# Loads and stores of the down weights' sums issued by GpSimd instead of SyncE, in the forgetting-attention loop of a YOCO-style trunk

## The chip, the cores and the metric

The kernel runs on one core of one Trainium2 chip. The metric is the device time of one execution in microseconds (us), the median of three runs. A core has five engines with instruction streams of their own: TensorE (PE in the profile, with its weight loads as PEld), VectorE (DVE), ScalarE (ACT), GpSimd (POOL) and SyncE (SP). In this kernel DMAs are issued by SP and by POOL; each of the two has a queue of its own, and all transfers share the core's 16 DMA engines. An instruction that waits holds up everything behind it on its engine.

## What is computed

Two layers of a decoder trunk over 512 tokens of width 1024: a dilated windowed attention with a gated ConvFFN, then a shared key/value projection, the forgetting attention (FoX) and a second ConvFFN. The change lies in the loop of the forgetting attention. Cut to that:

```python
def fox_mixer(xn, w_q, w_o, k, v, c):
    q = (xn @ w_q).reshape(B, T, B_HEADS, HEAD_DIM)          # 16 heads of 64
    for i in range(T // BLK):                                # 4 blocks of 128 queries
        s = einsum(q[block], k[:prefix]) * scale
        s = s + (c_t[:, :, q0:q1, None] - c_t[:, :, None, :q1])   # forget bias
        s = where(causal, s, NEG)
        p = softmax(s)
        outs.append(einsum(p, v[:prefix]))
    return concat(outs) @ w_o

def conv_ffn(xn, w_up, cw, cb, w_down):
    ...
    return (gelu(gate) * val) @ w_down
```

The kernel's second ConvFFN needs, besides `w_down` itself, differences of blocks of `w_down` (the "down weights' sums"). They depend on nothing but the weights, so they are made ahead, during the attention loop, and kept in a DRAM tile `dT[1]`.

## The kernel before, in words

**The loop.** 16 heads are taken as 8 pairs j = 0..7, and the 4 query blocks as two halves (i0 = 0 and 2), which makes 16 *steps* m = 0..15: step m works on j = m // 2 and i0 = 0 (m even) or 2 (m odd), each step with two sub-steps a = 0, 1 (query block i = i0 + a). Two more rounds (m = 16, 17) drain the pipeline. In one step PE does scores (L1715, `s_ps`), the probability-value products of step m - 2 (L1762, `o_ps`), four parts of the next heads' query projection (`q_part`, through `mm3` L277 to L279, `q_ps`) and the transposes of step m - 1's probabilities (L1747, `pT_ps`). DVE adds the bias and finds the minimum (L1723), ACT does the exponential (L1725), DVE divides (L1735), ACT copies the transposes (L1749).

**The bias.** `f_bias` (L1690 and after) runs on POOL, one step ahead: for each sub-step two TENSOR_SCALARs (L1696) and one AFFINE_SELECT (L1697). The first bias of an even step has 128x384 operands, its second one 128x512; in an odd step they are 128x128 and 128x256. They read `ck`, a broadcast copy of the cumulative gate for pair j, 512 KB, which SP loads at the start of each even step (L1492).

**The weights.** Products are done in three passes with a high and a low part of each weight. Query weights come in pieces of 512 KB: SP loads `wraw` (L49); ACT writes the high part (L57) and the negated high part (L59, `high(minus=True)`, end of an even step); then, in the next odd step, POOL issues a DMA that *adds* `wraw` onto the negated part, which gives the low part (`low_added`, L82). This is called the **accumulate** below. The accumulate issued in odd step m is used by PE in step m + 1, sub-step 1: in `q_part` the first product of the group that needs the low part is L279. So the accumulates of steps 1, 3, 5, 7, 9 are wanted in steps 2, 4, 6, 8, 10; that of step 11 belongs to the output projection and is wanted later.

**The sums.** `sums_between(l, j)` is a generator: it loads 1 MB of `w_down` in three DMAs (L1783 512 KB, L1784 and L1785 256 KB each) into a tile `dsums`, then on DVE makes four subtractions (L1787, L1788; L1790, L1791), then stores 1 MB into `dT` (L1793). Four of them run in the loop, for j = 2..5, started at m = 2, 6, 10, 14:

```python
for j, m in ((2, 2), (3, 6), (4, 10), (5, 14)):
    g = sums_between(1, j)
    for i in ((m, 1), (m + 1, 2), (m + 2, 0), (m + 2, 1)):
        sums[i] = g
```

so the loads stand at (m, sub-step 1), the subtractions at the end of step m + 1 and in step m + 2, sub-step 0, and the store at (m + 2, sub-step 1); all of m, m + 2 are even. In the loop's body `next(sums.get((m, a), idle))` comes right behind `f_bias` and `q_part` of that sub-step.

**What sets the order.** The program is scheduled by hand: each engine's order is the order of the code. Tiles come from pools with a fixed number of buffers (`t4`: 10 of 4 KB a partition, for `wraw`, `ck` and `bias`; `t8`: 16 of 8 KB, for `w`, `dsums` and others), so an instruction that fills a tile also waits for the last readers of what the buffer held. The second bias of an even step gets the buffer of the `wraw` that the preceding accumulate reads, and so waits for that accumulate to land.

Of the kernel before, what the change touches and what calls it, by code (L numbers as in the profile page):

```python
# [101 lines left out]
def trunk_kernel(ctx, tc, x, norm_gains, w_qkv_a, w_o_a, w_q_b, w_o_b, kv_norm, w_kvf, b_f,  # L102
                 w_up, conv_w, conv_b, w_down, rope, out):
    nc = tc.nc
    act, dve, pool, pe, sp = nc.scalar, nc.vector, nc.gpsimd, nc.tensor, nc.sync
# [8 lines left out]
    def t8(shape, dt=F32, name="t8"):  # L114
        return p8.tile(shape, dt, tag="t8", name=name)
# [47 lines left out]
    dT = [tc.dram_tile([ND, 128, 2048], F32, name=f"dT{l}") for l in range(2)]  # L163
# [1472 lines left out]
    for bp in range(2):  # L1636
        for s in range(2):
            t = slice(bp * 128, bp * 128 + 128)
# [139 lines left out]
    def sums_between(l, j):  # L1778

        t = t8([128, 2, 1024], name="dsums")  # L1780
        a, b = t[:, 0], t[:, 1]
        r = w_down[l][j * 256:j * 256 + 256, :].rearrange("(c p) d -> c p d", p=128)
        sp.dma_start(a, r[0])  # L1783
        sp.dma_start(b[:, 0:512], r[1, :, 512:1024])  # L1784
        sp.dma_start(b[:, 512:1024], r[1, :, 0:512])  # L1785
        yield
        dve.tensor_tensor(a[:, 0:512], a[:, 512:1024], a[:, 0:512], ALU.subtract)  # L1787
        dve.tensor_tensor(a[:, 512:1024], b[:, 0:512], a[:, 512:1024], ALU.subtract)  # L1788
        yield
        dve.tensor_tensor(b[:, 0:512], b[:, 0:512], a[:, 0:512], ALU.subtract)  # L1790
        dve.tensor_tensor(b[:, 512:1024], b[:, 512:1024], b[:, 0:512], ALU.subtract)  # L1791
        yield
        sp.dma_start(dT[l][j].rearrange("p (q d) -> p q d", q=2), t)  # L1793
        yield

    pairs = [(j, i) for j in range(8) for i in (0, 2)]
# [13 lines left out]
# [4 lines that stand above are left out]
    for m in range(M + 2):  # L1814
        live = m < M
        if live:
            j, i0 = pairs[m]
# [91 lines left out]
```

## Time and profile before

| | |
|---|---|
| median of 3 runs | 1118.66 us (1118.03 to 1118.78) |
| the profiled execution's own time | 1118.55 us |
| its span (first to last instruction) | 1116.8 us, so 1.75 us lie around it |
| busy: PE, PEld, DVE, ACT, POOL | 1100.9, 949.9, 895.5, 660.8, 212.8 us |
| mean granted TensorE clock | 0.996 |
| the attention loop's steps in the trace | about 619 to 737 us |
| DMA moved | 237.32 MB, mean 213 GB/s |

The page gives shares of the whole span. The change touches some 110 us of it, so the views that matter are those cut to that stretch: the waits of one engine, its instructions in order of time, the chain of work that ended last, and the busy time of each engine and of the DMA engines in windows. In a row of the instruction view stand start, duration, engine, line, operation and tiles, and in square brackets the idle time before it with what ended it. In a row of the windows stand the window, its length, the busy time of PE, PEld, DVE, ACT and POOL (with instruction counts), the granted clock, the DMA engines' mean busy share and GB/s.

### The profile page before, as it was taken

The page shows a single profiled execution, that of the slowest core. Times are in us where ns is not written, and L with a number is a line of the kernel's source. Part 1 is how long each engine was busy: PE and PEld are TensorE (multiplying, and loading weights), DVE is VectorE, ACT ScalarE, POOL GpSimd, SP SyncE. Part 2 cuts the span into 40 slices and gives each one's busy share as a digit, 9 for nine tenths or more (in the row PEclk, how much of TensorE's full clock was granted, in tenths as well). Part 3 has the DMA queues.
Part 4 walks back from the last instruction along what each step waited for, and adds up shares of the span by engine and source line. Part 5 has one row for each costly group of instructions (what it writes and reads, how often), then busy time and mean ns, then how long its engine had stood idle before and what let it go on. Part 6 is the DMA issues. An engine that isn't in the chain of part 4 may idle for free.

```text
span 1116.8 us, 18134 instructions
## 1 busy us (share of the span) xinstructions
PE 1100.9 (99%) x6611; PEld 949.9 (85%) x6611; DVE 895.5 (80%) x1494; ACT 660.8 (59%) x1092; POOL 212.8 (19%) x313
## 2 busy tenths in 40 slices
PE   9999999999999999999999899999999999999997
PEld 6988889899999988887988677788989999988886
DVE  6667778878888799997877577858978877799995
ACT  5444565656556557476555577756565565557473
POOL 1832101111111111000110555500211111111000
PEclk9999999999999999999999899999999999999999
DMA  9469854468788989794882666583457889899862
GB/s 324 151 216 407 334 163 134 112 148 192 187 183 201 297 303 337 264 336 78 206 183 64 207 190 190 169 244 101 119 141 176 197 206 217 234 319 334 314 245 76
DMA packets 185075, 237.32 MB, mean 213 GB/s; under 512 B 11737, under 2 KB 131529, under 8 KB 184474
## 3 DMA queue, kind: packets, MB, share of 16 engines
q1 hardware_dynamic: 169274, 185.00, 51.0%
q0 software_dynamic: 15712, 51.16, 20.9%
q8 instruction: 52, 0.85, 0.3%
q14 instruction: 37, 0.30, 0.1%
HBM read 170.28 MB, written 39.63 MB: 188 GB/s over the span
## 4 chain that ended last, share of the span: by engine, by line
PE 84%; issue 6%; DMA 4%; ACT 3%; DVE 2%; POOL 1%; DVEq 0%; POOLq 0%; ACTq 0%; SPq 0%
PE up L278 13%; PE up L277 13%; PE up L279 13%; PE acc L278 8%; PE acc L277 8%; PE acc L279 8%; DMA w<-wraw 3%; PE qk_ps L278 2%; PE qk_ps L277 2%; PE qk_ps L279 2%; PE first L279 1%; PE first L277 1%; PE first L278 1%; PE v_ps L277 1%; PE v_ps L279 1%
## 5 line engine op out<-in xcount | busy, mean ns | idle before, releaser
L277 PE MATMUL acc<-w 128*128 128x512 f32 (+1 forms) x311 | 120.5, 388 | 0.0
L279 PE MATMUL acc<-w 128*128 128x512 f32 (+1 forms) x311 | 120.4, 387 | 0.0
L57 ACT CAST w<-wraw 128x1024 fp32r<-128x1024 f32 x96 | 99.1, 1048 | 14.1 <-DMA wraw<-in_w_o_b_dram 5.3
L278 PE MATMUL acc<-w 128*128 128x512 f32 (+1 forms) x267 | 103.3, 387 | 0.0
L65 DVE TENSOR_TENSOR w<-wraw,w 128x1024 fp32r<-128x1024 f32 x66 | 88.2, 1351 | 18.4 <-ACT w L57 17.8
L641 ACT ACTIVATE bb<-up,conv 128x512 f32<-128x512 f32 x80 | 60.0, 775 | 67.4 <-DVE up L1022 42.8
L278 PE MATMUL up<-xbl,w 128*128 128x512 f32 (+1 forms) x280 | 96.3, 344 | 0.0
L278 PE MATMUL up<-xcl,w 128*128 128x512 f32 (+1 forms) x280 | 96.3, 344 | 0.0
L277 PE MATMUL up<-xch,w 128*128 128x512 f32 (+1 forms) x280 | 96.3, 344 | 0.0
L277 PE MATMUL up<-xbh,w 128*128 128x512 f32 (+1 forms) x280 | 96.3, 344 | 0.0
L279 PE MATMUL up<-xch,w 128*128 128x512 f32 (+1 forms) x280 | 96.2, 344 | 0.0
L279 PE MATMUL up<-xbh,w 128*128 128x512 f32 (+1 forms) x280 | 96.2, 344 | 0.0
L279 PE MATMUL up<-xsh,w 128*128 128x256 f32 x320 | 90.6, 283 | 0.0
L277 PE MATMUL up<-xsh,w 128*128 128x256 f32 x320 | 90.6, 283 | 0.0
L278 PE MATMUL up<-xsl,w 128*128 128x256 f32 x320 | 90.6, 283 | 0.0
L277 PEld LDWEIGHTS acc<-w 128*128 128x128 f32 x311 | 58.4, 188 | 12.0
L279 PEld LDWEIGHTS acc<-w 128*128 128x128 f32 x311 | 58.4, 188 | 11.8
L644 DVE SCALAR_TENSOR_TENSOR bb<-up,conv,bb 128x510 f32<-128x510 f32 x80 | 59.9, 749 | 2.8
L277 PEld LDWEIGHTS up<-xsh,w 128*128 128x128 f32 x320 | 61.4, 192 | 0.0
L278 PEld LDWEIGHTS up<-xsl,w 128*128 128x128 f32 x320 | 61.4, 192 | 0.0
L279 PEld LDWEIGHTS up<-xsh,w 128*128 128x128 f32 x320 | 61.4, 192 | 0.0
L642 DVE SCALAR_TENSOR_TENSOR bb<-up,conv,bb 128x511 f32<-128x511 f32 x80 | 59.4, 742 | 2.6 <-ACT bb L641 2.6
(333 smaller groups left out, 3154.2 us busy)
## 6 DMA issues: line engine op xcount, KB each, us to landing
wraw<-in_w_up_dram SPq DMA_DIRECT2D x88, 512.0 KB, 5.2
w<-wraw POOLq DMA_DIRECT2D x50, 512.0 KB, 6.0
dT<-dsums SPq DMA_DIRECT2D x24, 512.0 KB, 6.5
dsums<-in_w_down_dram SPq DMA_DIRECT2D x22, 512.0 KB, 5.4
dsums<-in_w_down_dram SPq DMA_DIRECT2D x44, 256.0 KB, 7.2
hD<-hc POOLq DMA_DIRECT2D x44, 256.0 KB, 7.8
dact<-hD SPq DMA_DIRECT2D x44, 256.0 KB, 5.6
wraw<-dT SPq DMA_DIRECT2D x22, 512.0 KB, 6.6
```

Source lines behind the costliest of these rows:

```text
L57: self.nc.scalar.copy(pair[:, 0], raw)
L65: self.nc.vector.tensor_tensor(pair[:, 1], raw, pair[:, 0].bitcast(F32), ALU.subtract)
L277: pe.matmul(o, ah, bh, start=first, stop=False, skip_group_check=shared)
L278: pe.matmul(o, ah, bl, start=False, stop=False, skip_group_check=shared)
L279: pe.matmul(o, al, bh, start=False, stop=last, skip_group_check=shared)
L641: act.activation(bb[:, s, :], ps, AF.Identity, bias=cp[:, 3, ch:ch + 1], scale=cp[:, 2, ch:ch + 1])
L642: dve.scalar_tensor_tensor(bb[:, s, 1:], ps[:, :T - 1], cp[:, 1, ch:ch + 1], bb[:, s, 1:], ALU.mult, ALU.add)
L644: dve.scalar_tensor_tensor(bb[:, s, 2:], ps[:, :T - 2], cp[:, 0, ch:ch + 1], bb[:, s, 2:], ALU.mult, ALU.add)
```

## The change

The four DMA issues of `sums_between` go from `sp` to `pool`; the generator's places in the loop stay. It runs four times, so 12 loads (4 MB) and 4 stores (4 MB) move.

```diff
@@ sums_between
-        sp.dma_start(a, r[0])
-        sp.dma_start(b[:, 0:512], r[1, :, 512:1024])
-        sp.dma_start(b[:, 512:1024], r[1, :, 0:512])
+        pool.dma_start(a, r[0])
+        pool.dma_start(b[:, 0:512], r[1, :, 512:1024])
+        pool.dma_start(b[:, 512:1024], r[1, :, 0:512])
...
-        sp.dma_start(dT[l][j].rearrange("p (q d) -> p q d", q=2), t)
+        pool.dma_start(dT[l][j].rearrange("p (q d) -> p q d", q=2), t)
```

PE, DVE and ACT keep their order to the instruction. On SP, from the query weights' and `ck`'s loads of step 2 on, the rows before are:

```order
L49 DMA wraw<-in_w_q_b_dram 128x8x128
L1492 DMA ck<-cd 128x1024
L1783 DMA dsums<-in_w_down_dram 128x1024
L1784 DMA dsums<-in_w_down_dram 128x512
L1785 DMA dsums<-in_w_down_dram 128x512
L49 DMA wraw<-in_w_q_b_dram 128x8x128
L1492 DMA ck<-cd 128x1024
L1793 DMA dT_76<-dsums 128x2048
L49 DMA wraw<-in_w_q_b_dram 128x8x128
L1492 DMA ck<-cd 128x1024
```

and of the change, from the same row on:

```order
L49 DMA wraw<-in_w_q_b_dram 128x8x128
L1492 DMA ck<-cd 128x1024
L49 DMA wraw<-in_w_q_b_dram 128x8x128
L1492 DMA ck<-cd 128x1024
L49 DMA wraw<-in_w_q_b_dram 128x8x128
L1492 DMA ck<-cd 128x1024
```

The loads and the store are gone from between SP's other loads; a `wraw` load that stood behind a store now stands behind a `ck` load.

On POOL, from the biases of step 2 (rows L1696 and L1697) over the accumulate of step 3 (L82) to that of step 5, the rows before are:

```order
L1696 TENSOR_SCALAR bias<-ck,cq 128x512 x2
L1697 AFFINE_SELECT bias<-bias 128x2x128
L82 DMA w<-wraw 128x1024
L1696 TENSOR_SCALAR bias<-ck,cq 128x128 x2
L1697 AFFINE_SELECT bias<-bias 128x2x128
L1696 TENSOR_SCALAR bias<-ck,cq 128x256 x2
L1697 AFFINE_SELECT bias<-bias 128x2x128
L1696 TENSOR_SCALAR bias<-ck,cq 128x384 x2
L1697 AFFINE_SELECT bias<-bias 128x2x128
L1696 TENSOR_SCALAR bias<-ck,cq 128x512 x2
L1697 AFFINE_SELECT bias<-bias 128x2x128
L82 DMA w<-wraw 128x1024
```

and of the change, at its two ends (first the biases of step 2 and the accumulate of step 3, then the biases of step 4 and the accumulate of step 5):

```order
L1696 TENSOR_SCALAR bias<-ck,cq 128x512 x2
L1697 AFFINE_SELECT bias<-bias 128x2x128
L1783 DMA dsums<-in_w_down_dram 128x1024
L1784 DMA dsums<-in_w_down_dram 128x512
L1785 DMA dsums<-in_w_down_dram 128x512
L82 DMA w<-wraw 128x1024
```

```order
L1696 TENSOR_SCALAR bias<-ck,cq 128x512 x2
L1697 AFFINE_SELECT bias<-bias 128x2x128
L1793 DMA dT_76<-dsums 128x2048
L82 DMA w<-wraw 128x1024
L1696 TENSOR_SCALAR bias<-ck,cq 128x128 x2
L1697 AFFINE_SELECT bias<-bias 128x2x128
```

The loads stand between the second bias of an even step and the next accumulate, and so does the store two steps later. From step 12 on there is no accumulate behind them: the store of step 12 stands ahead of the biases of step 13, and the loads of step 14 and the store of step 16 end POOL's part of the loop.

## The prediction

> **What bounds the kernel now.** The page's first part says that PE is busy 1100.9 of 1116.8 us, so only what stops or slows PE can be won. Next I read who PE waited for in the stretch that the change touches (620 to 700 us), and then those waits in PE's order of time; in the waits' rows stand the total, the count and the longest.
>
> ```profile
> PE 1100.9 (99%) x6611; PEld 949.9 (85%) x6611; DVE 895.5 (80%) x1494; ACT 660.8 (59%) x1092; POOL 212.8 (19%) x313
> ...
> PE q_ps L279 <- DMA w<-wraw: 6.5, 3, 4.9
> ```
>
> ```profile
> 637.83 0.79 PE L279 MATMUL q_ps<-xqh,w 128*128 128x512 f32 x1 [4.91 <-DMA w<-wraw]
> ...
> 653.36 0.40 PE L279 MATMUL q_ps<-xqh,w 128*128 128x512 f32 x1
> ...
> 667.29 0.50 PE L279 MATMUL q_ps<-xqh,w 128*128 128x512 f32 x1 [0.83 <-DMA w<-wraw]
> ...
> 680.33 0.40 PE L279 MATMUL q_ps<-xqh,w 128*128 128x512 f32 x1
> ...
> 694.67 0.50 PE L279 MATMUL q_ps<-xqh,w 128*128 128x512 f32 x1 [0.74 <-DMA w<-wraw]
> ```
>
> These five rows are the first products that need the accumulated low part, in steps 2, 4, 6, 8 and 10. Three wait (4.91, 0.83, 0.74 us, together 6.48), and the two of steps 4 and 8 don't. The first wait costs more than itself: in the windows the granted clock is at half behind it.
>
> ```profile
> 636.30:643.20 6.90, 5.37 (x22) 4.45 (x24) 0.19 (x1) 2.14 (x4) 1.78 (x3) 0.51 0.23 73
> ```
>
> From one such product to the next takes 653.36 - 637.83 = 15.53 us there, and 680.33 - 667.29 = 13.04 two pairs of steps later at full clock, where nothing waited either: the half clock cost 15.53 - 13.04 = 2.5 us. So 9.0 us hang on these three accumulates. The chain of waits has them with start and length, and the accumulates of all five steps stand on POOL:
>
> ```profile
> 627.36 10.42 DMA w<-wraw
> ...
> 658.49 8.75 DMA w<-wraw
> ...
> 685.22 9.41 DMA w<-wraw
> ```
>
> ```profile
> 644.43 0.90 POOL L82 DMA_DIRECT2D w<-wraw  x1 [4.71 <-ACT w L59]
> ...
> 672.28 0.88 POOL L82 DMA_DIRECT2D w<-wraw  x1 [3.10 <-ACT w L59]
> ```
>
> The three that PE waits for took 8.75 to 10.42 us. How long one takes alone is seen in the windows behind 644.43, where it is the only transfer:
>
> ```profile
> 646.00:647.00 1.00, 1.00 (x6) 0.78 (x5) 0.63 (x4) 1.00 (x4) 0.93 (x3) 1.00 1.06 205
> 647.00:648.00 1.00, 1.00 (x7) 0.87 (x6) 1.00 (x2) 0.58 (x2) 0.93 (x3) 1.00 1.07 201
> 648.00:649.00 1.00, 1.00 (x7) 0.70 (x6) 1.00 (x3) 0.00 (x0) 1.00 (x3) 1.00 0.38 70
> 649.00:650.00 1.00, 1.00 (x15) 0.83 (x15) 0.97 (x2) 0.59 (x1) 0.93 (x2) 1.00 0.00 0
> ```
>
> The DMA engines fall idle at 648.4, 4.0 us after the issue; with 0.5 us until PE sees it (10.42 for the first, whose engines fell idle some 0.5 us before) it lands in about 4.5 us. What stands beside the slow ones is on SP:
>
> ```profile
> 625.98 0.32 SPq L1492 DMA_DIRECT2D ck<-cd  x1
> 626.40 0.38 SPq L1783 DMA_DIRECT2D dsums<-in_w_down_dram  x1
> ...
> 627.30 0.42 SPq L1785 DMA_DIRECT2D dsums<-in_w_down_dram  x1
> 628.52 0.38 SPq L49 DMA_DIRECT2D wraw<-in_w_q_b_dram  x1
> ...
> 653.44 0.33 SPq L1793 DMA_DIRECT2D dT<-dsums  x1
> 653.93 0.38 SPq L49 DMA_DIRECT2D wraw<-in_w_q_b_dram  x1
> 655.46 0.32 SPq L1492 DMA_DIRECT2D ck<-cd  x1
> 655.83 0.64 SPq L1783 DMA_DIRECT2D dsums<-in_w_down_dram  x1
> ...
> 683.10 1.03 SPq L1783 DMA_DIRECT2D dsums<-in_w_down_dram  x1
> ```
>
> SP has nothing else to do, so it runs ahead and sends the 1 MB of loads as soon as the buffer is free: 1.0, 2.7 and 2.1 us ahead of the accumulates of steps 1, 5 and 9, though their place in the code is a step later. The accumulates of steps 3 and 7 have no such load beside them. That is the collision.
>
> **The change part by part.**
>
> *Where the loads go.* On POOL they stand behind the second bias of steps 2, 6, 10 and 14, and that bias waits for the accumulate before it:
>
> ```profile
> 637.88 1.37 POOL L1696 TENSOR_SCALAR bias<-ck,cq 128x512 f32<-128x512 f32 x2 [4.84 <-DMA w<-wraw]
> ...
> 667.33 1.37 POOL L1696 TENSOR_SCALAR bias<-ck,cq 128x512 f32<-128x512 f32 x2 [3.32 <-DMA w<-wraw]
> 668.78 0.41 POOL L1697 TENSOR_SCALAR_AFFINE_SELECT bias<-bias 128x256 f32<-128x256 f32 x1
> ```
>
> So a load can no longer be in flight beside the accumulates of steps 1, 5 and 9; it starts 1.9 us after they land (667.33 to 669.19).
>
> *Step 2.* How much of 1 MB's time comes off the first accumulate? The neighbouring row is that of a window in which a copy fills the engines:
>
> ```profile
> 733.00:734.00 1.00, 1.00 (x8) 0.92 (x7) 0.00 (x0) 0.82 (x2) 0.00 (x0) 1.00 0.97 393
> ```
>
> At 393 GB/s 1 MB is 2.7 us. Between 627 and 637 us the engines had no gap, so taking out 2.7 us of work brings the landing from 637.8 to 635.1 if the accumulate still ends last. If it shares evenly with `ck` and the one `wraw` that stay, it ends before them, at about 633.9. PE wants it at 637.83 - 4.91 = 632.92, so 1.0 to 2.2 us of wait stay; I take 1.8, nearer to the first, since in all three cases the accumulate ended with the last of its neighbours. Gain 4.91 - 1.8 = 3.1 us. The half clock began about 3.4 us into the wait (636.3); a wait of 1.8 us (the other two of 0.83 and 0.74 left the clock at 1.00) should not bring it: 2.5 us more. The Trainium skill ("TensorE: Matmul & The Clock Gate", Part 1) says that the clock halves after an idle window of some 3.4 us and that the window runs freely; by that rule a wait of 1.8 us can't contain one, and this trace agrees.
>
> *Steps 6 and 10.* Without the loads the accumulates of 658.49 and 685.22 have `ck` ahead, nearly done, and a `wraw` late in their time. PE wants them at 667.29 - 0.83 = 666.46 and 693.93, 8.0 and 8.7 us after issue; alone they need 4.5, and 2.7 less than 8.75 and 9.41 is 6.1 and 6.7. Both waits go: 1.57 us.
>
> *Steps 4 and 8, which are late next.* Their accumulates now have 1 MB ahead on their own queue. They are wanted 653.36 - 644.43 = 8.9 and 680.33 - 672.28 = 8.05 us after issue, need 4.5, and so have 3.5 to 4.4 us to spare. The loads start 3.1 us ahead of them (669.19 to 672.28) and move 2.7 us, with `ck` (512 KB, half of that) beside them: 1 to 2 us of delay, which fits. POOL's issue time is the unknown one:
>
> ```profile
> L657 POOL DMA_DIRECT2D hD<-hc x42 | 33.6, 800 | 6.8 <-DVE hc L659 6.8
> L1532 POOL DMA_DIRECT2D wraw<-in_w_kvf_dram x8 | 9.9, 1240 | 106.5 <-DVE vr L321 54.9 <-DVE w L1537 24.8 <-DVE xf L484 24.5
> L615 POOL DMA_DIRECT2D dT<-dsums x12 | 6.5, 544 | 8.6 <-DVE dsums L610 4.5 <-DVE dsums L608 3.9
> ```
>
> No row has a plain load on POOL. Between 544 and 1240 ns each, three cost 1.6 to 3.7 us; I take 0.54 + 2 x 0.80 = 2.1, since the shapes are those of L615 and L657. It is hidden by the 3.10 us in which POOL waits for ACT's L59 anyway; at 3.7 us the accumulate goes out 0.6 us later, inside the spare time. Cost 0 (below zero it can't be, as POOL is not waited for there).
>
> *The subtractions.* DVE takes them up where they stand, at 648.60 and 676.45:
>
> ```profile
> 648.60 0.86 DVE L1787 TENSOR_TENSOR dsums<-dsums 128x512 f32<-128x512 f32 x1
> ...
> 676.45 0.85 DVE L1787 TENSOR_TENSOR dsums<-dsums 128x512 f32<-128x512 f32 x1
> ```
>
> The second stands 9.2 us behind PE's 667.29. The loads start 1.9 us behind the landing and end after 1 us of issue, 2.7 + 1.3 us of transfer and 0.5 us of notice, at 7.4: 1.8 us to spare in step 3, where the accumulate before lands latest, and more later. Cost 0; if DVE waited, all of steps 4 and 5 would wait with it.
>
> *The stores.* They wait for the same subtraction on POOL as on SP, behind a bias that is done by then, and POOL's next work is the accumulate 5.0 us later (653.44 to 658.49); one store costs 0.5 to 1.2 us of issue. Only in step 12 are biases queued behind, for a step later, and POOL has idle time after those:
>
> ```profile
> 715.32 2.61 POOL L1696 TENSOR_SCALAR bias<-ck,cq 128x384 f32<-128x384 f32 x2 [4.11 <-ACT pT L1749]
> ```
>
> They come 1 to 2 us later, within those 4.11. SP's `wraw` of 653.93 no longer stands behind the store and goes some 4 us earlier, into a gap. Cost 0.
>
> *Sum.* 3.1 + 2.5 + 1.57 = 7.1 us, taken from PE's own idle and slow time and carried to the end, since PE is full from 720 us on. The profiled execution took 1118.55 us, 0.11 below the median: 1118.55 - 7.1 = 1111.4.
>
> **The rivals.**
>
> *The first wait goes wholly.* If the accumulate lands before 632.9 (it needs 4.5 us alone, which would be 631.9), all 9.0 us come: 1109.6. Against it: `ck` and a `wraw` stay beside it.
>
> *The first wait stays.* If the accumulate's pace is set by `ck` and `wraw`, and more than 3.4 us of wait remain, the half clock stays too: 1.5 + 1.57 = 3.1 us at most, near 2.4 on the whole: 1116.1. For it: the accumulate got only some third of the engines' time in all three collisions.
>
> *The collision moves, and it is slower.* The loads and the accumulates of steps 3 and 7 now share one queue. If the loads are slow there, PE waits in steps 4 and 8 instead. It decides from 8 us between issue and landing on, which the three slow accumulates all passed. With 12.5 us both would cost what step 2 cost, 4.9 + 2.5 each: 1118.55 - 7.1 + 14.8 = 1126.3; even is at about 3.5 us of wait in each. Against it: the loads start 3.1 us ahead and no other transfer of that size is there. The Trainium skill ("SBUF — State Buffer", section "SBUF: two separate sides", the box on the "DVE blocks DMA" trap and the paragraphs after it) speaks for it: a DMA issued by GpSimd can stand until a VectorE operation in a two-port mode ends, 620 ns becoming 3100. By that, three loads would take 9 us and this rival would hold. In this trace POOL issued the twelve L615, between DVE's subtractions, at a mean of 544 ns, so I see no sign of it.
>
> That the change does nothing is excluded by SP's and POOL's order: the loads can't go ahead of the accumulate.
>
> **How the numbers follow.** A measurement of this kernel can tell about 0.2% (2.2 us) from no change: below 1116.4 is faster. Forecast (1110.5 to 1114) 0.62; first wait goes 0.13; first wait stays 0.15, split by that bound, 0.08 faster and 0.07 same; collision moves 0.10, of which 0.01 ends within the bound. Faster 0.83, same 0.08, slower 0.09. The range takes in the second case and most of the third: 1108.8 to 1116.6.
>
> **What the profile would show.** Right: L279's wait in step 2 falls from 4.91 to 1 to 2.2 us, those of steps 6 and 10 vanish, no half clock near 640, POOL's loads follow a 128x512 bias, the accumulates of steps 5 and 9 land in under 7 us. Wrong: PE or DVE waiting in steps 4 or 8 for `w` or `dsums`, or POOL's loads lasting over 1.5 us each.

## The result, and the profile after

The changed kernel takes **1110.33 us** (median of 6 runs, 1109.79 to 1110.87); the kernel before, run beside it, 1118.61 (6 runs, 1118.01 to 1118.78). The ratio is 0.9927, with a 95% interval of 0.9914 to 0.9940: 8.3 us saved, where 7.1 were forecast. The time lies inside the range, but 0.2 us below the main case's 1110.5 to 1114, between it and the case in which the first wait goes wholly (1109.6). The profiled execution of the changed kernel took 1110.27 us, with a span of 1108.5 and a mean granted clock of 0.998 (before 1118.55, 1116.8 and 0.996).

The page's first part and PE's waits from 612 to 740 us, after the change (in the waits' rows: total, count, longest):

```profile
PE 1098.4 (99%) x6611; PEld 948.4 (86%) x6611; DVE 896.6 (81%) x1494; ACT 660.2 (60%) x1092; POOL 222.2 (20%) x329
```

```profile
PE q_ps L279 <- DMA w<-wraw: 0.8, 1, 0.8
PE acc L278 <- DVE w L65: 0.8, 1, 0.8
```

The three waits for accumulates, 6.5 us, are one of 0.8. POOL is 9.4 us busier and has 16 instructions more, the moved issues; no wait of PE or DVE in this stretch ends on them. PE's first products of steps 2, 4, 6, 8 and 10 with the accumulated part, in order of time:

```profile
633.99 0.50 PE L279 MATMUL q_ps<-xqh,w 128*128 128x512 f32 x1 [0.83 <-DMA w<-wraw]
...
647.04 0.40 PE L279 MATMUL q_ps<-xqh,w 128*128 128x512 f32 x1
...
660.48 0.40 PE L279 MATMUL q_ps<-xqh,w 128*128 128x512 f32 x1
...
673.42 0.40 PE L279 MATMUL q_ps<-xqh,w 128*128 128x512 f32 x1
...
686.85 0.40 PE L279 MATMUL q_ps<-xqh,w 128*128 128x512 f32 x1
```

Steps 6 and 10 no longer wait, and steps 4 and 8 still don't. From step 2 to step 4 it is 647.04 - 633.99 = 13.05 us, against 15.53 before. The granted clock (third number from the end of a window's row) says why:

```profile
631.00:637.00 6.00, 5.17 (x35) 4.09 (x35) 2.79 (x12) 4.10 (x13) 5.01 (x11) 1.00 0.57 119
637.00:643.00 6.00, 6.00 (x56) 4.68 (x54) 4.91 (x15) 5.15 (x13) 4.45 (x9) 1.00 0.95 298
```

The half clock of 636.30 to 643.20 is gone. POOL's rows show the moved issues, and the first accumulate stands in the chain of waits:

```profile
634.04 1.38 POOL L1696 TENSOR_SCALAR bias<-ck,cq 128x512 f32<-128x512 f32 x2 [0.77 <-DMA w<-wraw]
635.49 0.41 POOL L1697 TENSOR_SCALAR_AFFINE_SELECT bias<-bias 128x256 f32<-128x256 f32 x1
635.84 0.58 POOL L1783 DMA_DIRECT2D dsums<-in_w_down_dram  x1
...
638.93 0.90 POOL L82 DMA_DIRECT2D w<-wraw  x1 [1.41 <-ACT w L59]
...
646.19 2.13 POOL L1696 TENSOR_SCALAR bias<-ck,cq 128x512 f32<-128x512 f32 x2 [0.98 <-DMA w<-wraw]
...
648.90 0.60 POOL L1793 DMA_DIRECT2D dT<-dsums  x1
652.16 0.87 POOL L82 DMA_DIRECT2D w<-wraw  x1 [2.66 <-ACT w L59]
...
658.70 1.44 POOL L1696 TENSOR_SCALAR bias<-ck,cq 128x512 f32<-128x512 f32 x2 [1.02 <-DMA w<-wraw]
```

```profile
627.59 6.35 DMA w<-wraw
```

The loads follow a 128x512 bias that waited for the accumulate, and start 1.9 us after it landed (635.84 against 627.59 + 6.35 = 633.94). The first accumulate took 6.35 us instead of 10.42.

### The profile page after: what moved, and what is told of

Its sections match the earlier page's. It is cut to its first block, busy times and chain, and to the rows that moved or that the text cites. A ratio compares the mean times of both kernels' runs of the same rounds, so it can differ in the third digit from the quotient of the medians.

```text
span 1108.5 us, 18139 instructions
## 1 busy us (share of the span) xinstructions
PE 1098.4 (99%) x6611; PEld 948.4 (86%) x6611; DVE 896.6 (81%) x1494; ACT 660.2 (60%) x1092; POOL 222.2 (20%) x329
## 4 chain that ended last, share of the span: by engine, by line
PE 89%; DVE 3%; issue 3%; ACT 2%; DMA 2%; POOL 1%; DVEq 0%; POOLq 0%; ACTq 0%
PE up L278 13%; PE up L277 13%; PE up L279 13%; PE acc L278 8%; PE acc L277 8%; PE acc L279 8%; PE qk_ps L278 2%; PE qk_ps L277 2%; PE qk_ps L279 2%; PE first L279 1%; PE first L277 1%; PE first L278 1%; PE o_ps L1762 1%; PE pT_ps L1747 1%; PE v_ps L278 1%
## 5 line engine op out<-in xcount | busy, mean ns | idle before, releaser
L65 DVE TENSOR_TENSOR w<-wraw,w 128x1024 fp32r<-128x1024 f32 x66 | 88.1, 1356 | 15.1 <-ACT w L57 14.7
```

What stands on the lines that cost most here:

```text
L65: self.nc.vector.tensor_tensor(pair[:, 1], raw, pair[:, 0].bitcast(F32), ALU.subtract)
```

## The experiments

Each kernel was timed in five rounds beside the kernel before, whose medians were 1117.90 (first four), 1117.77 (next four) and 1117.67 us (last three); all are single edits of the kernel before, or of the changed one where that is said.

### Loads alone, stores alone

```diff
@@ sums_between: the loads alone (the stores alone: the same for L1793 only)
-        sp.dma_start(a, r[0])
-        sp.dma_start(b[:, 0:512], r[1, :, 512:1024])
-        sp.dma_start(b[:, 512:1024], r[1, :, 0:512])
+        pool.dma_start(a, r[0])
+        pool.dma_start(b[:, 0:512], r[1, :, 512:1024])
+        pool.dma_start(b[:, 512:1024], r[1, :, 0:512])
```

Expected of the loads alone:

> Only the loads of the sums go to POOL, the stores stay on SP. Theory (what costs is the 1 MB of loads in flight beside the accumulates of steps 1, 5 and 9): nearly the whole gain, 1110.3 +- 0.8 us. Rival (what costs is that SP's queue is held up, its weight loads standing behind stores that wait for DVE): a part only, 1113 us or more.

and of the stores alone:

> Only the stores go to POOL, the loads stay on SP. Theory of the loads' collision: no change, 1118.6 +- 0.8 us, and PE's wait of 4.9 us in step 2 stays. Rival of SP's held-up queue: 1114 us or less.

Measured: loads alone 1110.96 us (1110.15 to 1111.36), ratio 0.9937 (0.9924 to 0.9951). Stores alone 1117.77 (1117.40 to 1119.25), ratio 1.0001 (0.9993 to 1.0010). PE's waits, first with the loads on POOL, then with the stores:

```profile
PE q_ps L279 <- DMA w<-wraw: 0.8, 1, 0.8
```

```profile
PE q_ps L279 <- DMA w<-wraw: 5.9, 3, 4.2
```

The loads make the gain; the stores are worth nothing that can be measured, and the weight loads that go earlier without them are not either.

### The first set alone, the others alone

```diff
@@ sums_between: the first set alone (the others alone: sp if j == 2 else pool)
+        q = pool if j == 2 else sp
-        sp.dma_start(a, r[0])
+        q.dma_start(a, r[0])
...
-        sp.dma_start(dT[l][j].rearrange("p (q d) -> p q d", q=2), t)
+        q.dma_start(dT[l][j].rearrange("p (q d) -> p q d", q=2), t)
```

> Loads and store of the first sums alone (step 2) go to POOL, those of steps 6, 10 and 14 stay on SP. Theory: the first wait (4.9 to 0.8 us) and its half clock (2.5 us) go, the waits of 0.83 and 0.74 us in steps 6 and 10 stay: 1118.6 - 6.6 = 1112.0 us. Rival (the three collisions are worth the same): 1118.6 - 8.3 / 3 = 1115.8 us.

> The complement: the first sums stay on SP, those of steps 6, 10 and 14 go to POOL. Theory: the wait of 4.9 us and its half clock stay, 1.57 us go: 1117.0 us. Rival (three equal collisions): 1118.6 - 2 x 8.3 / 3 = 1113.1 us.

Measured: the first set alone 1112.54 us, ratio 0.9954 (0.9942 to 0.9967); the others alone 1116.12 (1114.78 to 1117.24), ratio 0.9984 (0.9975 to 0.9993). PE's waits, the first set alone and then the others:

```profile
PE q_ps L279 <- DMA w<-wraw: 2.3, 3, 1.0
```

```profile
PE q_ps L279 <- DMA w<-wraw: 4.8, 1, 4.8
```

So 5.4 us hang on step 2 and 1.8 on steps 6 and 10 (by the terms of the prediction 5.6 and 1.57; the expectation of the first set alone, with the 0.83 us of wait that had been seen by then, was 6.6). In the trace of the first set alone each later wait is about as long as before; in the other it is the long one that stays. The parts add to 7.1 of the whole's 8.3, which the intervals (1.0 to 1.5 us each way) allow.

### The loads on SP, sent late: is it the engine or the time?

In the first kernel SP first issues a store of 64 bytes of the accumulated tile, which waits for the accumulate; the store's bytes go nowhere else. In the second the loads merely stand one sub-step later.

```diff
@@ sums_between, and the loop that places it (second kernel: the last line alone)
+        if j in (2, 3, 4):
+            sp.dma_start(seen[j:j + 1, :], qps[2 * j - 1][1][1][0:1, 0, 0:16].bitcast(F32))
         sp.dma_start(a, r[0])
...
-        for i in ((m, 1), (m + 1, 2), (m + 2, 0), (m + 2, 1)):
+        for i in ((m, 2), (m + 1, 2), (m + 2, 0), (m + 2, 1)):
```

> Nothing goes to POOL. On SP the loads of steps 2, 6 and 10 stand one place later (behind the step's weight load) and behind a store of 64 bytes that reads the accumulated weights of the step before, so that SP sends them only when that accumulate has landed. Theory (only the time of the loads counts, not the engine or queue that issues them): the gain of the change, 1110.3 +- 1 us, L279's wait in step 2 near 0.8 us. Rival (POOL's queue, on which loads and accumulates follow one another, is what helps): 1114 us or more, since on SP the loads now share the engines with the next accumulate and stand ahead of ck.

> Control for the run before: the same later place on SP, but no store that waits for the accumulate. SP still runs ahead, the loads go out about 2 us later than before, still beside the accumulate of step 1. Theory: 1116 to 1119 us, the wait in step 2 above 3 us. Rival (the place behind the weight load is what helps): 1110 to 1112 us.

Measured: behind the store 1110.22 us (1109.47 to 1111.09), ratio 0.9931 (0.9918 to 0.9943), the time of the changed kernel, with loads and stores all on SP. Which engine issues them, and on whose queue, thus doesn't matter.

The second was to be a control and went against what I expected: 1110.58 (1110.14 to 1110.75), ratio 0.9933 (0.9920 to 0.9947). SP's rows and the first accumulate in the chain show what happened there:

```profile
625.55 0.32 SPq L1492 DMA_DIRECT2D ck<-cd  x1
628.07 0.38 SPq L49 DMA_DIRECT2D wraw<-in_w_q_b_dram  x1
628.50 1.39 SPq L1783 DMA_DIRECT2D dsums<-in_w_down_dram  x1
629.94 1.55 SPq L1784 DMA_DIRECT2D dsums<-in_w_down_dram  x1
631.53 0.75 SPq L1785 DMA_DIRECT2D dsums<-in_w_down_dram  x1
```

```profile
626.93 6.53 DMA w<-wraw
```

One sub-step later in the code puts the loads behind the query weights' load, which waits for a buffer. So they were sent 1.6 us *after* the accumulate instead of 1.0 us ahead of it, and had been issued for five of its 6.53 us without harm. Two accounts are left: the loads must only start after the accumulate, or the weight load, now in front of them in the queue, shields it.

### The loads behind the accumulate, but ahead of the weights

From the kernel before: SP issues an eighth of the step's query weight load (which brings the wait for the buffer), then the three loads, then the other seven eighths.

```diff
@@ sums_between
+        n = W.n_dma
+        if j < 5:
+            raw = W.new_raw(n)
+            (dst, src), = W.pieces[n](raw)
+            k = dst.shape[1] // 8
+            sp.dma_start(dst[:, 0:k], src[:, 0:k])
         sp.dma_start(a, r[0])
...
+        if j < 5:
+            sp.dma_start(dst[:, k:], src[:, k:])
+            W.raw[n] = raw
+            W.n_dma += 1
```

> Kernel before, loads on SP at their old place in the code, but behind the first eighth of the step's weight load and ahead of its other seven eighths. The first eighth waits for the weights' buffer, so that the loads go out as late as in the control run (1 to 2 us behind the accumulate of step 1, not 1 us ahead of it). First account of the control run (the later start is what helps): about 1110.6 us again. Second account (it is the weight load in front of them on SP's ring that holds the loads' bytes back until the accumulate is nearly done): the loads' 1 MB is beside the accumulate again, a wait of 2 us or more in step 2, 1112.5 to 1117 us.

Measured: 1109.82 us (1109.16 to 1109.97), ratio 0.9927 (0.9915 to 0.9940). SP's rows, the first accumulate, and the DMA engines' share and GB/s (last two numbers) in the two windows around its landing:

```profile
628.77 0.33 SPq L1788 DMA_DIRECT2D wraw<-in_w_q_b_dram  x1
629.15 0.94 SPq L1789 DMA_DIRECT2D dsums<-in_w_down_dram  x1
...
632.11 0.65 SPq L1793 DMA_DIRECT2D wraw<-in_w_q_b_dram  x1
```

```profile
627.62 5.91 DMA w<-wraw
```

```profile
633.00:634.00 1.00, 0.60 (x3) 0.39 (x3) 0.74 (x4) 1.00 (x5) 0.67 (x2) 1.00 0.95 372
634.00:635.00 1.00, 1.00 (x8) 0.82 (x7) 1.00 (x2) 0.45 (x2) 1.00 (x2) 1.00 1.01 369
```

The weight load in front is not what protects it: with 64 KB of it ahead in place of 512, the accumulate landed in 5.91 us. The loads only have to come after it.

Whose bytes moved when is seen by queue: q1 is SP's, q0 is POOL's, on which only the accumulate was under way. The rows give packets, MB and the share of the 16 engines' time. In the kernel before, from the accumulate's issue at 627.36 to 632.5, and then from 633 to 636 us:

```profile
q1 hardware_dynamic: 407, 1.21, 87.9%
```

```profile
q0 software_dynamic: 131, 0.48, 80.9%
q1 hardware_dynamic: 275, 0.18, 22.6%
```

With the loads sent 1.5 us behind it, from 629 to 632 us:

```profile
q0 software_dynamic: 122, 0.50, 99.5%
q1 hardware_dynamic: 35, 0.05, 5.1%
```

So the two did not share the engines evenly in either kernel. In the kernel before, the accumulate moved nothing for 5.1 us after its issue (alone, the one of step 3 had its first packets within 1.6), while SP's queue, with `ck` and the loads sent ahead of it, moved 1.21 MB, 236 GB/s; then it moved. Here it moved first, and the loads, though issued from 629.15 on, came behind it, at some 370 GB/s once it had landed at 633.5. In the control run it was the same: 0.49 MB of the accumulate and 0.03 MB on SP's queue from 628.5 to 632.0.

### The loads in both places

The changed kernel, with the three loads issued on SP at the old place as well (and then again on POOL).

```diff
@@ sums_between (changed kernel)
+        sp.dma_start(a, r[0])
+        sp.dma_start(b[:, 0:512], r[1, :, 512:1024])
+        sp.dma_start(b[:, 512:1024], r[1, :, 0:512])
         pool.dma_start(a, r[0])
```

> The changed kernel with the loads made twice: as before on SP into the same tile, and then again on POOL (4 MB more are read in all). Theory: the collision is back though POOL has all that the change gave it: wait in step 2 of 4 to 5 us and the half clock, 1117.5 to 1119.5 us. Rival (POOL's or SP's order is what counts, not the bytes in flight): 1110.3 to 1111.5 us.

Measured: 1118.02 us (1116.51 to 1118.84), ratio 0.9998 (0.9989 to 1.0007). The accumulates of steps 1, 5 and 9 in its chain:

```profile
627.27 10.00 DMA w<-wraw
...
657.65 8.97 DMA w<-wraw
...
684.63 9.89 DMA w<-wraw
```

The early loads alone bring back all that the change won, and the accumulates' old 9 to 10 us with it. This is the plainest proof that the collision was the cost.

### The half clock by itself

The kernel before, with PE kept busy through the long wait: the first product of that group is repeated 20 times ahead of itself, each into the same place, started anew.

```diff
@@ q_part
+        if j == 3 and i == 0:
+            for _ in range(20):
+                pe.matmul(o, wh[:, 0, :], xs(xTq, 0, ALL)[0], start=True, stop=True)
         for kc in (2 * i, 2 * i + 1):
```

> The kernel before, in which PE repeats a product of step 2 that needs only the high part 20 times (20 x 0.23 = 4.6 us of added work, its result overwritten), just ahead of the product that waits 4.9 us. Theory (the half clock behind the wait costs 2.5 us of its own): the added work fills the wait, the clock stays full, 1116.1 us. Rival (the half clock is hidden by the other engines, and the wait alone costs): 1118.6 us.

Measured: 1116.26 us (1114.81 to 1118.28), ratio 0.9990 (0.9981 to 0.9999). PE's rows, and the window behind them with the granted clock:

```profile
631.59 4.79 PE L1507 MATMUL q_ps<-xqh,w 128*128 128x512 f32 x20
...
636.68 0.39 PE L279 MATMUL q_ps<-xqh,w 128*128 128x512 f32 x1
...
649.60 0.40 PE L279 MATMUL q_ps<-xqh,w 128*128 128x512 f32 x1
```

```profile
637.00:660.00 23.00, 23.00 (x198) 18.36 (x198) 17.11 (x52) 17.00 (x41) 14.35 (x26) 1.00 0.59 161
```

Work of 4.79 us that nobody needs was added, and the kernel became 1.5 us faster by the medians: the wait was paid anyway, and the slow clock behind it was not. From step 2 to step 4 this trace takes 649.60 - 636.68 = 12.92 us where before it took 15.53, which is 2.6 us for the half clock. The medians give 1.5, the ratio 1.1 (0.1 to 2.1 by its interval), and the profiled execution is the fastest of the eleven: the mechanism is shown, its size on the whole kernel only so far.

### What the last 0.8 us wait for

Two edits of the changed kernel. In the first, SP's query weight load of step 2 waits for the accumulate, by a 64-byte store as above. In the second, the third set's last subtractions and store stand one step later.

```diff
@@ the loop, step m (first kernel)
+            if m == 2:
+                sp.dma_start(seen[0:1, :], qps[3][1][1][0:1, 0, 0:16].bitcast(F32))
...
@@ the loop that places the sums (second kernel)
-        for i in ((m, 1), (m + 1, 2), (m + 2, 0), (m + 2, 1)):
+        second = ((m + 3, 2), (m + 4, 0)) if j == 4 else ((m + 2, 0), (m + 2, 1))
+        for i in ((m, 1), (m + 1, 2), *second):
```

> The changed kernel, in which SP sends the weight load of step 2 only when the accumulate of step 1 has landed (a store of 64 bytes that reads its result stands in front). Theory (what is left of the first wait, 0.83 us, is that weight load beside the accumulate): the wait goes, 1109.5 us. Rival (the load is then late for ACT's L57, 2.5 us behind the wait): as the changed kernel or up to 1 us more, 1110.3 to 1111.5 us.

> The changed kernel, in which the second two subtractions of the third sums go from the start of step 12 to the end of step 13 and their store to step 14. Theory (PE's wait of 0.8 us for DVE's L65 in step 13 comes from those 1.9 us of subtractions ahead of it on DVE): the wait goes, 1109.5 us. Rival (ACT's exponentials set the pace of DVE there): 1110.3 us, no change.

Measured: 1110.76 us (1110.32 to 1110.99), ratio 0.9937 (0.9924 to 0.9951), and 1111.37 (1111.06 to 1112.81), ratio 0.9945 (0.9932 to 0.9957). Neither helped. The first kernel's windows and its PE:

```profile
631.00:632.00 1.00, 1.00 (x7) 0.81 (x6) 0.41 (x3) 0.39 (x3) 0.93 (x3) 1.00 0.62 115
632.00:633.00 1.00, 0.98 (x7) 0.55 (x5) 0.92 (x7) 0.94 (x4) 0.93 (x3) 1.00 0.06 12
```

```profile
633.72 0.50 PE L279 MATMUL q_ps<-xqh,w 128*128 128x512 f32 x1 [0.74 <-DMA w<-wraw]
```

My account, that this weight load holds up the accumulate, falls. Without it the DMA engines were all but idle from 632.0, yet PE got the tile at 633.7, about as late as with it (633.99). The accumulate's last 7 packets, 0.02 MB, are spread over 632.0 to 633.5; why they come so late is open. The later weight load also brought a new wait of 0.21 us in step 4.

In the second kernel PE's wait for the DVE group L65 (0.77 us in the changed kernel) all but went, and the next such group got a longer one:

```profile
706.42 0.50 PE L278 MATMUL acc<-w,OTb 128*128 128x512 f32 x1 [0.17 <-DVE w L65]
714.51 0.50 PE L278 MATMUL acc<-w,OTb 128*128 128x512 f32 x1 [1.63 <-DVE w L65]
```

The moved subtractions now run at 709.29 and 710.19, ahead of the L65 of 713.24 for which PE waits. So the theory was right for the wait that it named, but the move only put the subtractions in front of the next product; that they cause the second wait is likely by this order and not tested by itself.

## Why the prediction was right, point by point

**The collision** was the cause, as forecast: the early loads alone bring the loss back (1118.02), and the loads alone take it away (1110.96). The reason given for the cure, that a load "can no longer be in flight beside" the accumulates, was narrower than the truth: it may be issued while they run, if it is issued after them (1109.82), since its bytes then move behind theirs.

**Step 2** was the mis-sized term. 1.8 us of wait were left in the sum and 0.83 stayed, so it gave 4.08 and not 3.1; the wait also fell below the 1 to 2.2 us named as the sign of being right. I took 2.7 us off a landing at 637.8, as if the accumulate ended last among transfers that fill the engines; it landed 6.35 us after issue, 4.07 earlier, at 633.9. What was mis-sized is the price of the 1 MB: in the stretch in which the accumulate stood waiting, the engines moved 236 GB/s and not 393, and at that pace 1 MB takes 4.4 us. The other end of my bound, "about 633.9", is hit by luck: it was reckoned from even shares, and so was the "third of the engines' time" in the rivals, but by the rows of the queues the accumulate got nothing at first and most of the engines afterwards. Those of steps 5 and 9 were alike: no packet until 662.5 and 689.5, 4.0 and 4.3 us after issue.

**The half clock**: 2.5 us forecast, 15.53 - 13.05 = 2.48 in the two traces, 1.5 by the medians of the run that removed it alone. **Steps 6 and 10**: both waits went, 1.57 us, with accumulates that took 658.70 - 652.16 = 6.5 us (forecast 6.1) and, by POOL's rows, 6.2 (forecast 6.7). Together 4.08 + 2.5 + 1.57 = 8.15 of 8.3 us. (The forecast's own terms add to 7.17; it has 7.1.)

**Steps 4 and 8**: the accumulate of step 3 landed 646.19 - 638.93 = 7.3 us after issue, beside the moved loads; alone I had reckoned 4.5, with 1 to 2 us of delay. It was 2.8, more than forecast, and the room was smaller: PE wanted the tile 647.04 - 638.93 = 8.1 us after issue in the changed kernel, where I had read 8.9 in the kernel before. So 0.8 us were left, and the rival in which the collision moves, which begins at about 8 us, was nearer than I had it. (Its price was also off: with 12.5 us the waits would be 12.5 - 8.9 = 3.6 and 12.5 - 8.05 = 4.45 us, not 4.9 each.)

**POOL's issue time** was the unknown. In the changed kernel's rows of the tile `dsums` (count, then shortest, median and longest ns):

```profile
L1783 POOL DMA_DIRECT2D dsums<-in_w_down_dram x4: 570/584/645, 635.8 to 712.0; - x4
L1784 POOL DMA_DIRECT2D dsums<-in_w_down_dram x4: 547/564/569, 636.4 to 712.6; - x4
L1785 POOL DMA_DIRECT2D dsums<-in_w_down_dram x4: 563/563/597, 637.0 to 713.2; - x4
L1793 POOL DMA_DIRECT2D dT<-dsums x4: 542/596/600, 648.9 to 723.7; - x4
```

Three loads cost 1.7 us (forecast 2.1), a store 0.6 (0.5 to 1.2), and POOL still waited 1.41 us for ACT ahead of the accumulate, so the cover held. The trap in which a DMA issued by GpSimd stands behind VectorE's work, from the Trainium skill ("SBUF — State Buffer", section "SBUF: two separate sides"), has a DMA of some 620 ns take some 3100. Here the longest of the 16 issues took 645 ns, and the trace does not show it. **The subtractions** and **the stores** cost nothing, as forecast: PE has no wait for either, and the stores alone left the time the same within the interval.

## What to carry to other kernels

An engine with nothing else to do runs ahead, so a load goes out when its buffer is free and not where its line stands; before a transfer that somebody waits for, ask what such an engine has sent just ahead of it. What has to be changed is when the load starts, and any instruction that must wait anyway can hold it back: here one that waits for the accumulate on GpSimd, a 64-byte store on SP, or one place later in the code gave the same 7 to 8 us. A wait on TensorE that is long enough to halve the clock (here 4.9 us; waits of 0.8 were not) costs more than its length, so cut the longest wait first: 5.4 of the 8.3 us came from one.

## What the runs showed of the hardware

**Order among DMAs.** 1 MB of loads sent 1.0 us ahead of a 512 KB accumulate made it take 10.4 us; the same loads sent 1.5 us behind it left it at 5.9, beside 6.35 with no such load in flight. The issuing engine made no difference. In the kernel before, POOL's queue had no packet for 5.1 us after the accumulate's issue, while SP's moved 1.21 MB. The Trainium skill ("DMA: Bandwidth & Descriptors", section "Issuing engines are not separate DMA queues") says that engines share the same DMA engines and that a second issuer saves only the time of issue; these runs agree (1110.22 us with the late loads on SP, 1110.33 on POOL). Its section "Queues, rings and completion order" says that each DMA engine takes turns between queues, packet by packet. By even turns the loads on SP's queue would slow the accumulate on POOL's whenever both are in flight; the measurement shows that only when the loads came first. In other stretches both queues are served with about as many packets each (kernel before, 634 to 635 us: 46 on POOL's queue, 44 on SP's). Why the order of start decided here is not settled by these runs.

**The moved issues.** Plain loads issued by GpSimd cost it 0.55 to 0.65 us each, where the same loads took SP 0.38 to 1.03 us in the kernel before, and the kernel with all of them on SP was as fast.

**Useless work can pay.** 20 products in a wait of 4.9 us kept the granted clock at 1.00 and took 1.5 us off the kernel by the medians (0.1 to 2.1 by the interval).
